# A hybrid encoder on one core: the gates' logarithm moved behind k's convolutions, and an opening with products of ones

## The chip, the cores and the metric

The kernel runs on one core of a Trainium2 chip. The metric is the device time of one execution in microseconds (us), the median of three runs. Five engines work side by side, each through its own queue in order: TensorE (PE; its weight loads are listed apart as PEld), VectorE (DVE), ScalarE (ACT), GpSimd (POOL), and SyncE (SP), which here only issues transfers.

## The reference

A trunk of two layers over 256 tokens of 1024 channels, all in float32. Each layer:

```python
h = rmsnorm(x, norm_w[l]);  proj = h @ w_in[l]
q_a, k_a, v_a, ab_a, z_a, q_b, k_b, v_b, z_b, gate_a, gate_b = split(proj)
# branch a: five-tap convolution and SiLU on q_a, k_a, v_a; q, k of unit length, then
beta = sigmoid(ab[:2])                                  # two directions, eight heads
g = -exp(a_log) * softplus(ab[2:] + dt_bias)            # logarithms of the decays
g = cumsum(g within a chunk)
decay = where(lower, exp(g_i - g_j), 0)
L = where(strict, (kb @ k.T) * decay, 0);  T = inverse(eye + L)   # gated delta rule, both directions
# branch b: differential attention, with rotary positions
lam = exp(sum(lp[0] * lp[1])) - exp(sum(lp[2] * lp[3])) + lambda_init
a = softmax(s0) - lam * softmax(s1)
x = x + (sigmoid(gate_a) * (y_a @ w_pa) + sigmoid(gate_b) * (y_b @ w_pb)) @ w_out
```

A final rmsnorm closes the trunk.

## The kernel before

**Tiling.** Tokens lie in two tiles of 128 rows (`m`, or `c` for chunk; `NM = 2`). A projection takes 512 columns of weights at a time, in four pairs `kp` of row blocks (`kt = 2 kp + k`). Every weight tile `raw` (128 x 1024 float32) is loaded by SP, cast by ScalarE into an upper part `hi` (L308), and VectorE writes the rest, the lower part `lo` (L310). The activations `hT` have an upper and a lower part too, and each product is three: upper x upper, upper x lower, lower x upper. `hi` and `lo` have two buffers, so that a cast waits until TensorE has left the tile before the last.

**The opening (layer 0).** Five products of ones run while the first loads come in; the norm's weights are spread by three products (`norm_row`), then the positions are turned by two 1x1 products into `pos_p` (L435). `opening` norms row tile 0, turns it (`rows`, `split_T`: four transposes each for channels 0 to 511 and 512 to 1023, a ScalarE cast at L234, a VectorE subtraction at L238), and begins the first half of `v_b`'s projection with `products(m, kp, lower)` (L454). An order written by hand ties them together: `mark["proj"]` is the last product, and `behind(x)` queues an instruction behind `x` on the same engine. With `lower` false a pair gives four products, upper and lower activations with upper weights; with `lower` true two, upper activations with lower weights. Between the two pairs of row tile 0 the second row tile is normed and turned.

**A layer's order.** Then come the small parameters, the 32 columns of `ab` (gates), the exponential of their negative size (`ev`, L635), λ (`ls`, L647; `neglam`), k's convolutions in two halves of four heads (`conv`: the copy at L666, four tap steps on VectorE at L670, a Tanh at L676, a product at L681; then transposes and squares), the second half of `v_b`'s projection (`proj_by_tile`, tile `pp_vb`, L369), q's convolution, and q's and k's projections of the attention (`pp_qk`). `v_b`'s second half, row tile by row tile, takes two of four PSUM banks that k's convolutions use as well. One of its weight tiles lies in the place that `B` takes later.

**The gates.** `log_decays()` stands behind `v_b`'s second half. It adds to k's sums of squares (`kss`, which lie beside `ev` in one tile `e_`), takes POOL's power for the lengths (L730), one logarithm over all 40 columns (L732), and makes from them `lnc` (bias of the exponentials) and `glog`; four products with `tri` sum `glog` along the tokens (`grps`, L745); VectorE copies the sums to `grow`, POOL sends them to DRAM (`gdr`), four transposes turn them (`gcps`), and `ngc`, `E_`, `nE` follow. `decays(g, c)` then, for each of four groups of heads and chunk, has POOL fetch `gdr` spread over 128 partitions into `B` (L780), adds `kds`, masks both directions with `affine_select` (L786), and has ScalarE take eight exponentials (L791) with `lnc` as bias; `weigh_k(g, c)` adds the directions and multiplies by k k^T (`kk`, L772, on TensorE). An order `cut` holds the last two fetches behind a mask.

The scheduler takes instructions in the order in which the program names them as their priority, so that a step named earlier goes first where its inputs are there; `behind` and `issue_after` bind it further.

Of the kernel before, what the change touches and what calls it, by code (L numbers as in the profile page):

```python
# [17 lines left out]
P = 128  # L18
# [31 lines left out]
def hybrid_encoder(  # L50
# [219 lines left out]
    def behind(ins):  # L270
        return nullcontext() if ins is None else tc.issue_after(ins)
# [161 lines left out]
    pos_p = ps_p.tile([P, 512], F32, tag="p", name="pos")  # L433
    for m in range(NM):
        mm = T.matmul(pos_p[:, m : m + 1], pos_r[:, m * P : (m + 1) * P], ones[0:1, 0:1], start=True, stop=True)  # L435
        tc.keep_in_program_order(mm)

    def opening(w, evac, places):

        accs = banks2("pp_vb00")
        later, lows = {}, []
        parts = weights(w, C_VB, 512, "vb00", places, ahead=False, later=later, spare=(3,), halved=(0,), late=lows)
        ws = [next(parts), next(parts)]
        tokens(1)

        def products(m, kp, lower):
            terms = [(2 * kp + k, pa, 0) for k in range(2) for pa in range(2)]
            if lower:  # L450
                terms = [(2 * kp + k, 0, 1) for k in range(2)]
            for n_, (kt, pa, pw) in enumerate(terms):
                with behind(mark["proj"]):
                    mark["proj"] = T.matmul(accs[m], hT[kt // 4][:, pa, kt % 4, m * P : (m + 1) * P], ws[kt][1 + pw],  # L454
                                            start=kt == 0 and not n_ and not lower,
                                            stop=kt == KT - 1 and lower).ins

        def rows(m, i, h, **kw):
            split_T(hT[i], heads4(h[:, 512 * i : 512 * i + 512]), m, f"h0{i}", bank_c, **kw)
            mark["turn", m, i], mark["split", m, i] = mark["turn"], mark["split"]  # L460

        h = normed(xt, wb, 0, "n0")
        low = mark["norm", 0][1]
        for high, lo, raw, hi in lows:
            with behind(low):
                low = V.tensor_tensor(lo, raw, hi, ALU.subtract).ins
        rows(0, 0, h, after=(None, low))
        made = norm_tiles("n0", 1)
        norm_factor(xt, 1, *made, range(2), mark["split", 0, 0][0])
        rows(0, 1, h, after=(mark["square", 1, 1], mark["sum"]))  # L470
        mark["proj"] = mark["turn", 0, 1]
        products(0, 0, False)
        products(0, 0, True)
        h = normed(xt, wb, 1, "n0", (None, mark["split", 0, 1][1]), made)
        later[1] = mark["split", 0, 1][0], mark["norm", 1][1]
        ws += [next(parts), next(parts)]
        products(0, 1, False)
        ws += [next(parts), next(parts)]
        at = mark["proj"]
        after = mark["vb00", 2]  # L480
# [12 lines left out]
        mark["later"] = {0: mark["vb00", 3]}  # L493


    for l in range(DEPTH):
# [152 lines left out]
        V.scalar_tensor_tensor(neglam, ls[:, 1:2], -lam0, ls[:, 0:1], ALU.add, ALU.subtract)  # L649


        kq = big.tile([P, NH, NM, 2, P], F32, tag="kq", name=f"kq{l}")
# [67 lines left out]
        gdr = dram.tile([NM, 8, 2, P], F32, tag="gdr", name=f"gdr{l}")  # L720
        lnc = small.tile([P, 2, NM, NH], F32, tag="lnc", name=f"lnc{l}")
        nE = small.tile([P, 4, NH], F32, tag="nE", name=f"nE{l}")
        E_ = small.tile([P, 4, NH], F32, tag="E_", name=f"E_{l}")

        def log_decays():
            kss = e_[:, :, 32:40]
            V.tensor_scalar(kss, ssk, 4.0 * EPS, None, ALU.add)
            kh = small.tile([P, NM, NH], F32, tag="kh", name=f"kh{l}")
            V.tensor_scalar(kh, kss, 1.0 / 16.0, None, ALU.mult)
            G.tensor_tensor(nrm.rearrange("p m h -> p (m h)"), kh.rearrange("p m h -> p (m h)"),  # L730
                            phalf, ALU.pow)
            S.activation(e_, e_, AF.Ln)  # L732
# [22 lines left out]
            ngc = small.tile([P, 4, NH], F32, tag="ngc", name=f"ngc{l}")  # L755
# [3 lines left out]
            V.tensor_tensor(lnc.rearrange("p d c h -> p (d c) h"), lnc.rearrange("p d c h -> p (d c) h"),  # L759
                            ngc, ALU.add)  # L760


        A = big.tile([P, 2, NM, 4, P], F32, tag="A", name=f"A{l}")
# [9 lines left out]
                                              start=True, stop=True).ins  # L773
            return heads4(gp)

        def decays(g, c, after=None):
            hs4 = slice(4 * g, 4 * g + 4)
            dec = B[:, c, hs4].rearrange("p h d i -> p d h i")
            with behind(after):
                G.dma_start(out=B[:, c, hs4].rearrange("p h d i -> p (h d i)"),  # L780
                            in_=gdr[c, hs4].rearrange("h d i -> (h d i)").partition_broadcast(P))
            end = (P - 1) * (1 - c)
            G.tensor_tensor(kds[:, c, hs4], dec[:, c, :, end], lnc[:, c, c, hs4], ALU.add)
            for d in range(2):
                sg = 1 - 2 * d
                mark["cut"] = G.affine_select(  # L786
                    out=dec[:, d], in_=dec[:, d], compare_op=ALU.is_ge, fill=BIG,
                    base=0, pattern=[[0, 4], [sg, P]], channel_multiplier=-sg).ins
                for j4 in range(4):
                    h = 4 * g + j4  # L790
                    S.activation(dec[:, d, j4, :], dec[:, d, j4, :], AF.Exp,  # L791
                                 bias=lnc[:, d, c, h : h + 1])
# [309 lines left out]
        qk_part(0, 0)  # L1102
        decays(0, 0)
        weigh_k(0, 0)
        cut = mark["cut"]
        decays(0, 1)
        weigh_k(0, 1)
        decays(1, 0, cut)
        weigh_k(1, 0)
        decays(1, 1, cut)  # L1110
        weigh_k(1, 1)
        turn_blocks()
        conv("q", C_QA, 1, 1)
# [238 lines left out]
```

## Time and profile before

| | |
|---|---|
| median of 3 runs | 751.38 us (750.87 to 751.71) |
| the profiled execution | 750.2 us |
| its span, first to last instruction | 748.5 us |
| mean granted TensorE clock | 0.997 |
| TensorE busy | 739.9 us (99%) |
| VectorE, ScalarE, POOL busy | 588.6, 475.3, 143.5 us |
| transfers | 135.45 MB, 181 GB/s in the mean |

In the profile a row of a timeline gives start, duration, engine, line, operation, tiles (out<-in), shape, count, and in brackets the idle time of the engine before it and what ended it. A float32 product of 128 x 128 stands in the records as two. Ends of matmuls are modelled, so that durations of neighbours overlap; the distance from start to start is what one costs.

### The profile page before, as it was taken

Reading aid. Unit: us, or ns where it says so; the run is one execution under the profiler, and the core shown is the slowest. Engines: PE = TensorE matmul, PEld = TensorE weight load, DVE = VectorE, ACT = ScalarE, POOL = GpSimd, SP = SyncE. Lnnn points to the kernel's source line nnn. Section 1 sums busy time; section 2 is a strip of 40 time slices with the busy share of each in tenths; the row PEclk is TensorE's granted clock in tenths of the full one; section 3 lists DMA queues with packets and bytes.
Section 4 is the critical chain, followed back from the end, with each engine's and each line's share of the span. In section 5 each row is a group of like instructions: output and inputs, shape, how many; then the busy total and the mean of one; then the engine's idle time right before and its main releaser. Section 6 shows DMA issues by size and latency. Waiting matters only on the chain.

```text
span 748.5 us, 13886 instructions
## 1 busy us (share of the span) xinstructions
PE 739.9 (99%) x5164; PEld 640.8 (86%) x5164; DVE 588.6 (79%) x1109; ACT 475.3 (64%) x1016; POOL 143.5 (19%) x221
## 2 busy tenths in 40 slices
PE   8999999999999999999999999999999999999996
PEld 6999889977888889888889889889778888998885
DVE  8686899999985965578667779999999679537782
ACT  6657675667876576645454677655687758566552
POOL 6000441112022450000000025202110425301000
PEclk9999999999999999999999999999999999999999
DMA  8752767776667462567674358768666747335641
GB/s 261 235 171 80 214 206 214 209 213 194 208 185 178 146 183 83 171 200 248 199 232 141 85 144 257 217 183 228 198 172 195 198 135 231 92 114 202 219 142 56
DMA packets 73733, 135.45 MB, mean 181 GB/s; under 512 B 12944, under 2 KB 13921, under 8 KB 73666
## 3 DMA queue, kind: packets, MB, share of 16 engines
q1 hardware_dynamic: 64750, 113.65, 50.0%
q0 software_dynamic: 7936, 19.35, 9.0%
q10 hardware_dynamic: 980, 1.58, 0.6%
q8 instruction: 40, 0.66, 0.4%
q14 instruction: 27, 0.22, 0.1%
HBM read 125.53 MB, written 9.01 MB: 180 GB/s over the span
## 4 chain that ended last, share of the span: by engine, by line
PE 97%; DMA 1%; issue 1%; DVE 0%; ACT 0%; SPq 0%; POOLq 0%; POOL 0%; DVEq 0%; ACTq 0%
PE pp_vb L369 4%; PE pp_qk L325 4%; PE pp_qk L324 4%; PE pp_qk L326 4%; PE sc L1033 2%; PE pp_o L369 2%; PE pp_za L325 2%; PE pf_v L385 2%; PE pf_k L385 2%; PE pf_v L389 2%; PE pp_gb L324 2%; PE pp_gb L325 2%; PE pp_zb L324 2%; PE pf_k L387 2%; PE pf_k L389 2%; PE pf_q L387 2%
## 5 line engine op out<-in xcount | busy, mean ns | idle before, releaser
L325 PE MATMUL pp_qk<-lo_qk,hT 128*128 128x512 f32 x128 | 50.7, 396 | 0.0
L326 PE MATMUL pp_qk<-hi_qk,hT 128*128 128x512 f32 x128 | 50.0, 390 | 0.0
L310 DVE TENSOR_TENSOR lo_qk<-raw_qk,hi_qk 128x1024 fp32r<-128x1024 f32 x32 | 39.5, 1234 | 9.6 <-ACT hi_qk L308 9.1
L324 PE MATMUL pp_qk<-hi_qk,hT 128*128 128x512 f32 x128 | 45.2, 394 | 0.0
L308 ACT CAST hi_qk<-raw_qk 128x1024 fp32r<-128x1024 f32 x28 | 29.4, 1049 | 23.6 <-PE pp_qk L326 11.8
L1043 ACT ACTIVATE es<-sc,mx 128x256 f32<-128x256 f32 x64 | 29.6, 474 | 19.6 <-DVE mx L1041 19.6
L310 DVE TENSOR_TENSOR lo_pb<-raw_pb,hi_pb 128x1024 fp32r<-128x1024 f32 x16 | 19.6, 1225 | 21.5 <-ACT hi_pb L308 21.2
L387 PE MATMUL pf_q<-hT,hi_q 128*128 128x256 f32 x128 | 36.2, 286 | 0.0
L385 PE MATMUL pf_q<-hT,hi_q 128*128 128x256 f32 x128 | 36.1, 286 | 0.0
L385 PE MATMUL pf_v<-hT,hi_v 128*128 128x256 f32 x128 | 35.8, 285 | 0.0
L385 PE MATMUL pf_k<-hT,hi_k 128*128 128x256 f32 x128 | 35.8, 285 | 0.0
L387 PE MATMUL pf_v<-hT,hi_v 128*128 128x256 f32 x128 | 35.8, 284 | 0.0
L387 PE MATMUL pf_k<-hT,hi_k 128*128 128x256 f32 x128 | 35.6, 283 | 0.0
L389 PE MATMUL pf_q<-hT,lo_q 128*128 128x256 f32 x128 | 34.8, 285 | 0.0
L389 PE MATMUL pf_v<-hT,lo_v 128*128 128x256 f32 x128 | 34.5, 287 | 0.0
L389 PE MATMUL pf_k<-hT,lo_k 128*128 128x256 f32 x128 | 34.3, 283 | 0.0
L670 DVE SCALAR_TENSOR_TENSOR cvq<-pf_q,cw,cvq 128x254 f32<-128x254 f32 (+1 forms) x64 | 29.9, 476 | 1.9 <-ACT cvq L666 1.4
L308 ACT CAST hi_pa<-raw_pa 128x1024 fp32r<-128x1024 f32 x16 | 16.9, 1054 | 22.2 <-PE pp_pa L326 16.0
L670 DVE SCALAR_TENSOR_TENSOR cvk<-pf_k,cw,cvk 128x254 f32<-128x254 f32 (+1 forms) x64 | 28.5, 478 | 2.1 <-ACT cvk L666 1.4
L670 DVE SCALAR_TENSOR_TENSOR cvv<-pf_v,cw,cvv 128x254 f32<-128x254 f32 (+1 forms) x64 | 29.7, 475 | 0.1
L325 PEld LDWEIGHTS pp_qk<-lo_qk,hT 128*128 128x128 f32 x128 | 24.0, 188 | 6.1 <-DVE lo_qk L310 1.3
L310 DVE TENSOR_TENSOR lo_pa<-raw_pa,hi_pa 128x1024 fp32r<-128x1024 f32 x16 | 19.6, 1224 | 11.2 <-ACT hi_pa L308 11.2
(409 smaller groups left out, 2541.2 us busy)
## 6 DMA issues: line engine op xcount, KB each, us to landing
raw_qk<-in_w_in_dram SPq DMA_DIRECT2D x32, 512.0 KB, 4.0
raw_k<-in_w_in_dram SPq DMA_DIRECT2D x16, 512.0 KB, 4.4
raw_q<-in_w_in_dram SPq DMA_DIRECT2D x16, 512.0 KB, 3.8
raw_v<-in_w_in_dram SPq DMA_DIRECT2D x16, 512.0 KB, 3.8
raw_zb<-in_w_in_dram SPq DMA_DIRECT2D x16, 512.0 KB, 3.9
raw_za<-in_w_in_dram SPq DMA_DIRECT2D x16, 512.0 KB, 3.8
raw_ga<-in_w_in_dram SPq DMA_DIRECT2D x16, 512.0 KB, 4.8
raw_pb<-in_w_pb_dram SPq DMA_DIRECT2D x16, 512.0 KB, 3.8
```

The source lines that it names most:

```text
L308: high = (V.tensor_copy if kp in turned else S.copy)(hi[:, :, :n], raw[:, :, :n]).ins
L310: mark[nm, kp] = high, V.tensor_tensor(lo[:, :, :n], raw[:, :, :n], hi[:, :, :n].bitcast(F32), ALU.subtract).ins
L324: T.matmul(o, act[kt // 4][:, 0, kt % 4, ts_], hi, start=kt == 0, stop=False)
L325: T.matmul(o, act[kt // 4][:, 0, kt % 4, ts_], lo, start=False, stop=False)
L326: mark["proj"] = T.matmul(o, act[kt // 4][:, 1, kt % 4, ts_], hi, start=False, stop=kt == KT - 1).ins
L369: mark["proj"] = T.matmul(o, act[kt // 4][:, pa, kt % 4, ts_], ws[kt][1 + pw], start=kt == 0 and n_ == 0, stop=kt == KT - 1 and n_ == 2).ins
L385: T.matmul(o, hi[:, cs], act[kt // 4][:, 0, kt % 4, :], start=first, stop=False, skip_group_check=True)
L387: T.matmul(o, hi[:, cs], act[kt // 4][:, 1, kt % 4, :], start=False, stop=False, skip_group_check=True)
L389: T.matmul(o, lo[:, cs], act[kt // 4][:, 0, kt % 4, :], start=False, stop=done, skip_group_check=True)
L670: V.scalar_tensor_tensor(ca[:, o0:o1], acc[:, b, o0 + sft : o1 + sft], cw[:, j, cb : cb + 1], ca[:, o0:o1], ALU.mult, ALU.add)
L1033: mm = T.matmul(sp[n][:, qt * SEQ : (qt + 1) * SEQ], qkT[h // 4][rows, 0, h % 4, qt * P : (qt + 1) * P], qkT[h // 4][rows, 1, h % 4, :], s ...
L1043: S.activation(es[:, n, qt, :], spv[:, qt, :], AF.Exp, bias=mx[:, n, qt : qt + 1], accum_out=s_all[:, h, n, qt : qt + 1])
```

## The change

*The opening.* Three products of ones with ones, written to unused columns of `pos_p`, stand ahead of the first transposes, and three more behind the first pair's products. The first pair of row tile 0 goes in another order: upper x upper for both row blocks, then upper activations x lower weights, then lower activations x upper weights.

*The gates.* `log_decays` is split. `gates()`, named behind k's convolutions, takes the logarithm of `ev` alone (queued behind the cast of the first weight tile of k's second half), `glog`, the sums, `gdr`, `ngc`, `E_`, `nE`. `lambdas()`, named behind `v_b`'s second half, takes λ's exponential (behind the cast of the second weight tile of k's second half). `spread()` issues the four fetches into `B` and then the eight masks in one go, ahead of `log_decays()`, which keeps k's sums, POOL's power, a logarithm of `kss` alone, and `lnc`. `decays` keeps `kds` and the exponentials, and the order `cut` is gone.

```diff
+        def warm(n):
+            for _ in range(n):
+                with behind(mark["proj"]):
+                    mark["proj"] = T.matmul(pos_p[:, P : 2 * P], ones, ones, start=True, stop=True).ins
+
+        mark["proj"] = mark["pos"]
+
         def products(m, kp, lower):
             terms = [(2 * kp + k, pa, 0) for k in range(2) for pa in range(2)]
-            if lower:
+            if lower is True:
                 terms = [(2 * kp + k, 0, 1) for k in range(2)]
+            elif lower:
+                terms = [(2 * kp + k, pa, pw) for k, pa, pw in lower]
...
+        warm(3)
         rows(0, 0, h, after=(None, low))
         made = norm_tiles("n0", 1)
         norm_factor(xt, 1, *made, range(2), mark["split", 0, 0][0])
         rows(0, 1, h, after=(mark["square", 1, 1], mark["sum"]))
         mark["proj"] = mark["turn", 0, 1]
-        products(0, 0, False)
-        products(0, 0, True)
+        products(0, 0, ((0, 0, 0), (1, 0, 0), (0, 0, 1), (1, 0, 1), (0, 1, 0), (1, 1, 0)))
+        warm(3)
...
-        S.activation(ls, ls, AF.Exp)
...
-            S.activation(e_, e_, AF.Ln)
-            V.scalar_tensor_tensor(ev, a_, 0.0, ev, ALU.max, ALU.add)
+            S.activation(kss, kss, AF.Ln)
             for d in range(2):
                 V.scalar_tensor_tensor(lnc[:, d], ev[:, :, d * 8 : d * 8 + 8], -1.0, kss,
                                        ALU.mult, ALU.subtract)
+            V.tensor_tensor(lnc.rearrange("p d c h -> p (d c) h"), lnc.rearrange("p d c h -> p (d c) h"),
+                            ngc, ALU.add)
+
+        def lambdas():
+            with behind(mark[f"k{l}1", 1][0]):
+                S.activation(ls, ls, AF.Exp)
+            V.scalar_tensor_tensor(neglam, ls[:, 1:2], -lam0, ls[:, 0:1], ALU.add, ALU.subtract)
+
+        def gates():
+            with behind(mark[f"k{l}1", 0][0]):
+                S.activation(ev, ev, AF.Ln)
+            V.scalar_tensor_tensor(ev, a_, 0.0, ev, ALU.max, ALU.add)
             glog = small.tile([P, NM, 16], F32, tag="glog", name=f"glog{l}")
...
+        def spread():
+            for g in range(2):
+                for c in range(NM):
+                    hs4 = slice(4 * g, 4 * g + 4)
+                    G.dma_start(out=B[:, c, hs4].rearrange("p h d i -> p (h d i)"),
+                                in_=gdr[c, hs4].rearrange("h d i -> (h d i)").partition_broadcast(P))
+            for g in range(2):
+                for c in range(NM):
+                    dec = B[:, c, 4 * g : 4 * g + 4].rearrange("p h d i -> p d h i")
+                    for d in range(2):
+                        sg = 1 - 2 * d
+                        G.affine_select(
+                            out=dec[:, d], in_=dec[:, d], compare_op=ALU.is_ge, fill=BIG,
+                            base=0, pattern=[[0, 4], [sg, P]], channel_multiplier=-sg)
...
         conv("k", C_KA, 0, 1)
+        gates()
         for _ in proj_by_tile(hT, wl, C_VB + 512, evac_v(1), f"vb{l}1", places2, spare=range(4),
...
             pass
+        lambdas()
+        spread()
         log_decays()
```

More of the change, by code (lines that the diff above doesn't have):

```diff
@@ L435, in hybrid_encoder @@
         mm = T.matmul(pos_p[:, m : m + 1], pos_r[:, m * P : (m + 1) * P], ones[0:1, 0:1], start=True, stop=True)
+        mark["pos"] = mm.ins
         tc.keep_in_program_order(mm)
@@ L454, in products @@
                     mark["proj"] = T.matmul(accs[m], hT[kt // 4][:, pa, kt % 4, m * P : (m + 1) * P], ws[kt][1 + pw],
-                                            start=kt == 0 and not n_ and not lower,
-                                            stop=kt == KT - 1 and lower).ins
+                                            start=kt == 0 and not n_ and lower is not True,
+                                            stop=kt == KT - 1 and lower is True).ins
         def rows(m, i, h, **kw):
@@ L722, in hybrid_encoder @@
         nE = small.tile([P, 4, NH], F32, tag="nE", name=f"nE{l}")
+        ngc = small.tile([P, 4, NH], F32, tag="ngc", name=f"ngc{l}")
         E_ = small.tile([P, 4, NH], F32, tag="E_", name=f"E_{l}")
@@ L754, in log_decays @@
                 T.transpose(gc_ps[:, dc * 8 : dc * 8 + 8], grow[:, dc, :], ident[:8, :8])
-            ngc = small.tile([P, 4, NH], F32, tag="ngc", name=f"ngc{l}")
             V.tensor_scalar(ngc, gc_ps[:, :32].rearrange("p (c h) -> p c h", c=4), -1.0, None, ALU.mult)
@@ L758, in log_decays @@
             V.tensor_scalar(nE, E_, -1.0, None, ALU.mult)
-            V.tensor_tensor(lnc.rearrange("p d c h -> p (d c) h"), lnc.rearrange("p d c h -> p (d c) h"),
-                            ngc, ALU.add)
         A = big.tile([P, 2, NM, 4, P], F32, tag="A", name=f"A{l}")
@@ L774, in gram, with decays @@
             return heads4(gp)
-        def decays(g, c, after=None):
+        def spread():
[12 more added lines that the diff above has]
+                            base=0, pattern=[[0, 4], [sg, P]], channel_multiplier=-sg)
+        def decays(g, c):
             hs4 = slice(4 * g, 4 * g + 4)
             dec = B[:, c, hs4].rearrange("p h d i -> p d h i")
-            with behind(after):
-                G.dma_start(out=B[:, c, hs4].rearrange("p h d i -> p (h d i)"),
-                            in_=gdr[c, hs4].rearrange("h d i -> (h d i)").partition_broadcast(P))
             end = (P - 1) * (1 - c)
@@ L784, in decays @@
             for d in range(2):
[L785 to L788, printed above, removed]
                 for j4 in range(4):
@@ L1104, in hybrid_encoder @@
         weigh_k(0, 0)
-        cut = mark["cut"]
         decays(0, 1)
         weigh_k(0, 1)
-        decays(1, 0, cut)
+        decays(1, 0)
         weigh_k(1, 0)
-        decays(1, 1, cut)
+        decays(1, 1)
         weigh_k(1, 1)
```

1 line of the change is left out of this document (removed).

## The prediction

> **What bounds the kernel now.** I read the page's busy line and chain, then who TensorE waited for, then the clock by stretches, then the opening engine by engine, then the stretch of k's and q's convolutions.
>
> ```profile
> PE 739.9 (99%) x5164; PEld 640.8 (86%) x5164; DVE 588.6 (79%) x1109; ACT 475.3 (64%) x1016; POOL 143.5 (19%) x221
> ...
> PE 97%; DMA 1%; issue 1%; DVE 0%; ACT 0%; SPq 0%; POOLq 0%; POOL 0%; DVEq 0%; ACTq 0%
> ```
>
> TensorE is 97% of the chain that ended last. Its waits for others, all of them in the list:
>
> ```profile
> PE idle L410 <- DVE ones L407: 1.1, 1, 1.1
> PE pp_vb L454 <- ACT hT L234: 0.4, 1, 0.4
> PE pp_vb L454 <- DVE hT L238: 0.3, 1, 0.3
> ```
>
> They sum to 1.8 us of a 748.5 us span, and all lie in the opening. So the gates, which the change moves, end no wait of TensorE: whatever leaves ScalarE or VectorE there comes off work that is hidden already. What the wait list can't show is a slow matmul. The stretches (columns: five engines' busy time, then granted clock, DMA share, GB/s) show one such place:
>
> ```profile
> 9.00:10.00 1.00, 0.65 (x3) 0.45 (x3) 0.57 (x2) 1.00 (x5) 0.00 (x0) 0.79 1.07 412
> 10.00:11.00 1.00, 1.00 (x4) 0.81 (x3) 0.74 (x3) 1.00 (x2) 0.87 (x2) 0.50 1.03 398
> ...
> 12.00:13.00 1.00, 1.00 (x4) 0.72 (x4) 1.00 (x2) 0.55 (x1) 1.00 (x1) 0.50 1.18 324
> 13.00:14.00 1.00, 1.00 (x10) 0.91 (x9) 1.00 (x2) 0.15 (x1) 1.00 (x1) 1.00 0.67 248
> ```
>
> The clock falls to half at 10.0 − 0.42 = 9.58 us (0.79 is 0.42 us at one half) and is back at 13.0: 3.4 us at half rate, which is 1.7 us of lost matmul time if nothing else had been late. The matmuls around it:
>
> ```profile
> 6.29 0.60 PE L435 MATMUL pos<-ones,pos_r 1*128 1x1 f32 x4
> 6.89 1.31 PE L227 MATMUL pt_h<-ident,h_n 128*128 128x128 f32 x8
> 8.62 0.49 PE L454 MATMUL pp_vb<-wA_vb,hT 128*128 128x512 f32 x1 [0.42 <-ACT hT L234]
> 9.46 2.42 PE L454 MATMUL pp_vb<-wA_vb,hT 128*128 128x512 f32 x5 [0.35 <-DVE hT L238]
> ...
> 13.21 1.04 PE L227 MATMUL pt_h<-ident,h_n 128*128 128x128 f32 x8
> 14.00 0.70 PE L454 MATMUL pp_vb<-wktm_vb,hT 128*128 128x512 f32 x2
> 14.54 1.55 PE L454 MATMUL pp_vb<-wvtm_vb,hT 128*128 128x512 f32 x6
> 15.93 0.39 PE L454 MATMUL pp_vb<-wA_vb,hT 128*128 128x512 f32 x1
> ```
>
> Between 6.3 and 9.4 us TensorE did the position's 1x1 products, eight transposes and one 128x512 product. In the slow stretch five 128x512 take 2.42 us with the last one's end, about 0.43 us from start to start; after it six take 15.93 − 14.54 = 1.39 us, 0.23 us each. From 14.54 on there is no gap.
>
> **The change, part by part. The opening, order of products.** Before, the second product needs the lower part of hT, so 8.62 to 9.46 holds one product. After, the upper parts of both rows and the lower parts of the weights go first: four products need only what is there at 8.62 and end near 9.5, when the lower part (8.73 + 0.68 = 9.41 below) is there. At full clock six products end at 8.62 + 6 × 0.23 = 10.0, against 9.46 + 5 × 0.43 = 11.6 before.
>
> ```profile
> 7.99 0.58 ACT L234 CAST hT<-pt_h 128x512 fp32r<-128x512 f32 x1
> 10.17 1.05 ACT L308 CAST wktm_vb<-raw_vb 128x1024 fp32r<-128x1024 f32 x1
> 8.73 0.68 DVE L238 TENSOR_TENSOR hT<-pt_h,hT 128x512 fp32r<-128x512 f32 x1
> 12.23 1.22 DVE L310 TENSOR_TENSOR wktm_vb<-raw_vb,wktm_vb 128x1024 fp32r<-128x1024 f32 x1
> 86.38 0.89 PE kk L772 x8
> ```
>
> The 1.7 us aren't all won. The next weights' upper part lands at 10.17 + 1.05 = 11.22, so the next four products run 11.27 to 12.2, the transposes (1.04 for eight, 13.21 to 14.25 by ends, 0.8 by starts) to about 13.1, and the next two wait for the lower part of that weight, 12.23 + 1.22 = 13.45. They then start at 13.48 where they started at 14.00: the gain is 0.5 us, and 0.6 us by the next group (13.95 for 14.54). VectorE is late next; it has work back to back there.
>
> **The opening, products of ones.** Two sets of three. Four fp32 128x128 products (two records each) took 0.89 us, so three cost 0.67 us at full clock. The first set starts when the position products are issued (6.29 + four steps of about 0.12 = 6.8) and ends at 7.45, so the transposes move from 6.89 to 7.45. ScalarE takes their result at 7.99, having been busy to then; the first four transposes would be readable near 8.2 (four starts of 0.11 us and some 0.3 us behind the last). That is 0.2 us later for everything in the opening, and the gain falls from 0.6 to 0.4 us. The second set fits between 10.2 and 11.4, where TensorE would wait for ScalarE: nothing, if the clock is up. Whether the filling holds the clock no row of before shows; bounds: yes, −0.6 (no delay of the transposes), and no, below. I take **−0.4 us**.
>
> The Trainium skill, "TensorE: Matmul & The Clock Gate", Part 1, says that a free-running window of 3413 ns decides between half and full rate, and that its phase varies from run to run; the 3.4 us above agree. Its Part 4 says transposes don't count as busy; if so, the filling is what decides.
>
> **The gates: ScalarE.** Before, one logarithm per layer takes 40 columns; after, one takes 32 (behind the first cast of the second half of k) and one 8 (in the old place). That puts a second pair of table loads into each layer, one before the new logarithm and one before the next Tanh. λ's Exp moves behind the logarithm; if it needs a load of its own, that is a third, which the Tanh load shares.
>
> ```profile
> 73.84 1.28 ACT L732 ACT_TABLE_LOAD   x1
> 75.13 0.27 ACT L732 ACTIVATE ge<-ge 128x80 f32<-128x80 f32 x1
> 76.68 1.28 ACT L676 ACT_TABLE_LOAD   x1
> ```
>
> So 2 × 1.28 + 0.2 = 2.8 us of ScalarE per layer, at this place:
>
> ```profile
> 36.50 0.48 ACT L666 ACTIVATE cvk<-pf_k,cw 128x256 f32<-128x256 f32 x1 [1.25 <-PE pf_k L389]
> 37.04 1.05 ACT L308 CAST hi_k<-raw_k 128x1024 fp32r<-128x1024 f32 x1
> 39.92 1.05 ACT L308 CAST hi_k<-raw_k 128x1024 fp32r<-128x1024 f32 x1 [0.88 <-PE pf_k L387]
> 41.37 0.42 ACT L676 ACTIVATE thk<-cvk 128x256 f32<-128x256 f32 x1 [0.40 <-DVE cvk L670]
> ...
> 38.13 1.23 DVE L310 TENSOR_TENSOR lo_k<-raw_k,hi_k 128x1024 fp32r<-128x1024 f32 x1
> ...
> 43.92 1.23 DVE L310 TENSOR_TENSOR lo_k<-raw_k,hi_k 128x1024 fp32r<-128x1024 f32 x1 [0.27 <-ACT hi_k L308]
> ...
> 49.89 1.22 DVE L310 TENSOR_TENSOR lo_q<-raw_q,hi_q 128x1024 fp32r<-128x1024 f32 x1 [0.78 <-ACT hi_q L308]
> ```
>
> The first load and the logarithm (1.5 us) fall into the 1.25 us idle before 36.50: 0.3 us late. The tile cast at 37.04 has its lower part at 38.13 + 1.23 = 39.36, and TensorE turns to it when it frees the buffer before (the cast at 39.92 waits for that): 0.6 us of slack, so no stall. The Tanh load falls before 41.37, into 0.4 us of idle: 0.9 us late. Here the queue behind counts: VectorE's next product for that head waits for the Tanh, and convolution steps of later heads stand behind it.
>
> The Trainium skill, "ScalarE: Activation LUTs", What ACT_TABLE_LOAD costs, puts a switch at 1283 ns and a drain of 1380 ns. By it the two loads would be an estimated 2.8 us longer per layer, and the sum, less the idle time and slack named here, about +2.5 us instead of −0.4. The trace differs: the load ends at 75.12, the logarithm starts at 75.13, with no drain, so that rule gets no chance of its own.
>
> **The gates: VectorE and TensorE.** Moved into k's stretch: five small operations of some 0.2 us, the copy of the sums' bank at 0.7 us, in all 1.6 us; the same leaves q's. TensorE's eight small fp32 records and eight transposes cost the same in either place. The tight spot is the second half of v's last product: its bank is k's second one, freed by the convolution of k's fourth head.
>
> ```profile
> 51.37 3.47 DVE L670 SCALAR_TENSOR_TENSOR cvk<-pf_k,cw,cvk 128x254 f32<-128x254 f32 x8
> 54.52 0.70 PE L369 MATMUL pp_vb<-wvb,hT 128*128 128x512 f32 x2
> ```
>
> Eight steps, alternating between the fourth head and the next half's first; the fourth head's last is the sixth, done two steps of some 0.45 us before 54.84, near 53.9: slack 0.6 us. VectorE's shift there is at most 0.9 + 1.6 = 2.5 us, less the 0.78 us of idle before 49.89 and 0.27 us before 43.92 = 1.45; less the slack, 0.85 us per layer (the second layer's work is the same), 1.7 in all. At the other end the moved operations wait behind k's steps and the price is zero. I take **+0.3 us** for both layers, nearer the low end, because no moved result is wanted before 60 us.
>
> **The gates: POOL, the transfers and what follows.**
>
> ```profile
> L791 ACT ACTIVATE B<-B,lnc 128x128 f32<-128x128 f32 x32 | 9.9, 391 | 1.3 <-POOL B L786 1.3
> L786 POOL TENSOR_SCALAR_AFFINE_SELECT B<-B 128x512 f32<-128x512 f32 x8 | 7.2, 916 | 0.0
> L325 PEld LDWEIGHTS pp_qk<-lo_qk,hT 128*128 128x128 f32 x32 | 6.0, 188 | 1.5 <-DVE lo_qk L310 0.4
> ...
> POOL nrm L730 <- DVE kh L729: 112.9, 2, 58.8
> ...
> 45.00:65.00 20.00, 20.00 (x127) 17.91 (x126) 15.74 (x35) 11.87 (x37) 0.00 (x0) 1.00 0.30 87
> 85.00:105.00 20.00, 20.00 (x152) 19.08 (x151) 18.11 (x32) 16.15 (x44) 9.91 (x14) 1.00 0.79 243
> ```
>
> Four broadcasts and eight masks (7.2 us) go ahead of the norm's power on POOL. POOL had idled 58.8 us before that power, whose result v's placing takes far later: nothing. On the transfer engines they leave a stretch at 0.79 for one at 0.30: nothing on SP's loads. The 32 exponentials (9.9 us) need not wait for them any more and can start near 77 instead of 91, spreading ScalarE's and VectorE's work out of the fullest 20 us (18.1 of VectorE). Weight loads of TensorE there waited 0.4 us for lower parts; at most that, 0.35 us per layer with the slowed matmuls, comes back. I take **−0.3 us** of 0 to −0.7.
>
> **Sum.** −0.4 + 0.3 − 0.3 = −0.4 us. On the profiled execution (750.2 us, a span of 748.5 and 1.7 around it): 749.8. The shown runs' median is 1.2 above it, so 751.0 there. A measurement of this kernel tells a change from none at about 0.2%, 1.5 us: 749.9 to 752.9 counts as the same.
>
> **The rivals.** *Slower, by VectorE's queue in k's stretch:* the Tanh load holds VectorE, the moved operations come before k's steps instead of behind, and v's second half starts late in both layers. 1.7 us as worked out; with a third load (1.28 us) or the sums' copy ahead of a weight's lower part (0.7 against 0.6 us of slack), another 0.3 to 0.5 per layer: +2.5 − 0.4 = 753.5. It decides once the shift reaches some 1.6 us per layer over what idle time takes up. For it: 18 of 20 us of VectorE's time are taken nearby. Against: 15.7 of 20 in this very stretch. Chance 0.18.
>
> *The clock falls all the same:* three products are too few. Then two of the six and the second set of ones run at half rate: 9.6 + 2.6 × 0.43 + 1.3 = 12.0, the four products end near 13.4, transposes 14.3, and the next group starts 0.2 us later than the old 14.54. +0.2 with the middle at nothing: 751.6. For it: 0.67 us of 3.4 is little. Against: the reordered products fill another 0.9 us of the same window. Chance 0.12.
>
> *Faster, by a half-rate stretch elsewhere:* a clock window that starts later would lay its 3.4 us over matmuls that nothing else holds up, and its removal is then worth the full 1.7 us, −1.9 in all with a little of the middle: 749.5. For it: the shown runs, 750.87 to 751.71, all lie above the profiled 750.2, by 0.7 to 1.5. Against: a window beginning after 9.5 holds back-to-back products and shouldn't be throttled. The free-running window of the Trainium skill (page and part named above) is this rule. Chance 0.18.
>
> **How the numbers follow.** Forecast as summed 0.52, own range 750.1 to 752.2. The point is its 751.0. The range reaches from the faster rival's 749.4 to 753.0, leaving out most of the slower one and a little below. Faster by over 0.2%: the faster rival and the rim of the forecast, 0.20; slower: the second, 0.18; the same: the rest, 0.62.
>
> **What would show it.** Right: a granted clock of 1.00 from 9 to 14 us, the wvtm group starting near 14.1, four table loads in each layer's k and q stretches, exponentials before 85 us, and TensorE's wait list no longer than before. Wrong: a TensorE wait at v's second half (near 54 and 420), weight loads waiting for lo_k or lo_q, or half rate in the opening.

## The result, and the profile after

The changed kernel takes 759.6 us (median of 4 runs, 758.0 to 761.9), the kernel before 751.1 beside it: a ratio of 1.0114, interval 1.0086 to 1.0142. It is 8.5 us slower; 751.0 was forecast, within 749.4 to 753.0.

The page of the changed kernel, busy line and chain:

```profile
PE 743.7 (98%) x5176; PEld 642.8 (85%) x5176; DVE 587.6 (78%) x1109; ACT 481.7 (64%) x1022; POOL 142.8 (19%) x221
...
PE 89%; DVE 4%; ACT 3%; DMA 2%; issue 2%; POOLq 0%; POOL 0%; DVEq 0%; ACTq 0%
```

ScalarE has 6.4 us more work, 5.1 of it four more table loads of 1.28 us, but it is busy for 64% of the span. What is not TensorE now holds 11% of the chain where it was 3%. What TensorE waited for (total, times, longest):

```profile
PE pf_q L385 <- ACT stg L597: 2.5, 2, 1.4
...
PE pp_qk L325 <- DVE lo_qk L310: 0.9, 3, 0.3
PE pf_q L389 <- DVE lo_q L310: 0.8, 1, 0.8
...
PE pf_q L385 <- ACT hi_q L308: 0.3, 1, 0.3
```

These new rows all lie in one place, the attention's q and k products (`pp_qk`) and q's second convolution half (`pf_q`). Comparing the starts of the same matmul in both traces: TensorE is 0.1 us early when q's convolution begins (60.2 us before), 3.9 late when v's begins (112.6), 4.7 at the end of the layer; in layer 1 it goes to 7.5 at v's convolution (478.5) and 8.6 at the end. Most of it, 6.8 us by these starts, is lost between q's first half and v's convolution (the list above counts idle time alone, 4.5 us there); 0.8 per layer is lost at the attention's score products, and is gone in every run below whose exponentials stand later.

ScalarE in that stretch of the changed kernel:

```profile
81.75 1.05 ACT L308 CAST hi_qk<-raw_qk 128x1024 fp32r<-128x1024 f32 x1 [0.66 <-PE pp_qk L326]
82.74 0.40 ACT L816 ACTIVATE B<-B,lnc 128x128 f32<-128x128 f32 x1
...
83.80 2.14 ACT L816 ACTIVATE B<-B,lnc 128x128 f32<-128x128 f32 x7
87.26 1.05 ACT L308 CAST hi_q<-raw_q 128x1024 fp32r<-128x1024 f32 x1 [1.32 <-DMA raw_q<-in_w_in_dram]
88.21 0.98 ACT L816 ACTIVATE B<-B,lnc 128x128 f32<-128x128 f32 x3
...
89.41 1.56 ACT L816 ACTIVATE B<-B,lnc 128x128 f32<-128x128 f32 x5
...
91.23 0.68 ACT L816 ACTIVATE B<-B,lnc 128x128 f32<-128x128 f32 x2
91.81 0.56 ACT L597 COPY stg<-pp_qk 128x512 f32<-128x512 f32 x1
```

and in the kernel before:

```profile
85.74 0.59 ACT L586 COPY stg<-pp_qk 128x512 f32<-128x512 f32 x1 [2.02 <-PE pp_qk L326]
...
91.51 1.27 ACT L791 ACTIVATE B<-B,lnc 128x128 f32<-128x128 f32 x4
```

Before, the copy `stg`, which frees a bank of `pp_qk`, ran the moment the products were done, and no exponential of `B` stood ahead of it. After, 18 of 32 stand ahead of it in ScalarE's program. TensorE's side in the changed kernel:

```profile
87.68 0.39 PE L326 MATMUL pp_qk<-hi_qk,hT 128*128 128x512 f32 x1
...
90.79 0.28 PE L389 MATMUL pf_q<-hT,lo_q 128*128 128x256 f32 x1
92.43 0.39 PE L385 MATMUL pf_q<-hT,hi_q 128*128 128x256 f32 x1 [1.36 <-ACT stg L597]
```

The products were done at 88.1; the copy started at 91.81, and the convolution wanted the bank near 91.1. The Trainium skill, "PSUM — Partial Sum Buffer", Engine vs sequencer instructions, says that ScalarE's queue is strictly first in, first out; these rows agree.

GpSimd's queue after:

```profile
69.89 1.16 POOL L771 DMA_DIRECT2D gdr<-grow  x2 [49.77 <-DVE grow L768]
75.24 2.21 POOL L797 DMA_DIRECT2D B<-gdr  x4 [4.19 <-DMA gdr<-grow]
...
86.69 0.49 POOL L812 TENSOR_TENSOR kds<-B,lnc 128x4 f32<-128x4 f32 x3
```

The sums reached DRAM only at 75 us, and the four fetches went out in a row. The stretches after (last columns: clock, DMA share, GB/s):

```profile
9.00:10.00 1.00, 1.00 (x4) 0.86 (x5) 0.67 (x1) 1.00 (x4) 0.00 (x0) 1.00 1.03 397
...
45.00:65.00 20.00, 20.00 (x127) 17.90 (x126) 15.66 (x35) 11.93 (x37) 0.00 (x0) 1.00 0.31 95
```

The clock's dip is gone. The stretch of few transfers is as it was (0.31): no fetch moved there. From 78 to 86 the transfer engines were full:

```profile
78.00:82.00 4.00, 4.00 (x23) 3.26 (x21) 2.52 (x4) 3.33 (x6) 3.92 (x3) 1.00 0.98 250
82.00:86.00 4.00, 3.67 (x15) 2.62 (x15) 3.96 (x9) 3.60 (x10) 2.90 (x5) 1.00 0.99 393
```

and in the kernel before:

```profile
78.00:82.00 4.00, 4.00 (x22) 3.00 (x21) 3.54 (x7) 2.06 (x4) 1.21 (x2) 1.00 0.56 174
82.00:86.00 4.00, 4.00 (x25) 3.21 (x25) 3.67 (x10) 1.74 (x4) 1.15 (x2) 1.00 0.64 164
```

The load of q's weights that SP issued at 76.69 us took 10.5 us to land; the same load took 4.4 before (issued at 75.33).

### The profile page after: what moved, and what is told of

The parts are those of the page before. It is cut to its first block, busy times and chain, and to the rows that moved or that the text cites. A ratio compares the mean times of both kernels' runs of the same rounds, so it can differ in the third digit from the quotient of the medians.

```text
span 757.1 us, 13925 instructions
## 1 busy us (share of the span) xinstructions
PE 743.7 (98%) x5176; PEld 642.8 (85%) x5176; DVE 587.6 (78%) x1109; ACT 481.7 (64%) x1022; POOL 142.8 (19%) x221
## 4 chain that ended last, share of the span: by engine, by line
PE 89%; DVE 4%; ACT 3%; DMA 2%; issue 2%; POOLq 0%; POOL 0%; DVEq 0%; ACTq 0%
PE pp_vb L369 4%; PE sc L1058 2%; PE pp_qk L324 2%; PE pp_qk L326 2%; PE pp_qk L325 2%; PE pp_o L369 2%; PE pp_zb L324 2%; PE pf_k L385 2%; PE pp_gb L325 2%; PE pp_za L325 2%; PE pp_gb L324 2%; PE pp_za L324 2%; PE pf_k L387 2%; PE pf_k L389 2%; PE pp_ga L324 2%; PE pp_ga L325 2%
## 5 line engine op out<-in xcount | busy, mean ns | idle before, releaser
L310 DVE TENSOR_TENSOR lo_qk<-raw_qk,hi_qk 128x1024 fp32r<-128x1024 f32 x32 | 39.6, 1237 | 10.7 <-ACT hi_qk L308 10.3
```

The lines of the kernel that those rows point to most:

```text
L310: mark[nm, kp] = high, V.tensor_tensor(lo[:, :, :n], raw[:, :, :n], hi[:, :, :n].bitcast(F32), ALU.subtract).ins
```

## The experiments

Each kernel is told from the kernel before ("before") or from the changed kernel ("after"); times are medians, ratios are to the kernel before on the same chip, with 95% intervals in brackets.

### Which half of the change

*The opening alone* (before, with the new opening):

```diff
+        warm(3)
         rows(0, 0, h, after=(None, low))
...
+        products(0, 0, ((0, 0, 0), (1, 0, 0), (0, 0, 1), (1, 0, 1), (0, 1, 0), (1, 1, 0)))
+        warm(3)
```

> The opening's part alone; the rest as before. The changed kernel's trace has the clock at full rate from 6.4 us on, yet TensorE stands only 0.1 us earlier at 18.8 us than before. Theory one (the rest alone makes the loss): 0 to -0.4 us, 750.7 to 751.1. Rival (the ones delay the first transposes, and that costs more in other phases of the clock's window): +0.5 us or more. Either way no wait at 80 to 100 us.

750.9 us, 1.0004 (0.9994 to 1.0014): nothing that shows.

*The gates alone* (after, with the old opening):

> The gates' part alone; the opening as before. If the loss lies wholly there: 759 to 761 us, with TensorE 4.7 us late at z's projections and 8.7 us late at the end, and the same waits near 82 to 92 us. If opening and gates only lose together (the earlier TensorE meets a late cast), it would come to 752 to 755.

759.7 us, 1.0118 (1.0103 to 1.0134): all of it.

### Which step of the gates, one taken back at a time

*Fetches two by two, masks between:*

```diff
         for g in range(2):
             for c in range(NM): G.dma_start(...)
-        for g in range(2):
             for c in range(NM): ... G.affine_select(...)
```

> The changed kernel, but the fetches of B go two by two, the masks of the first pair ahead of the second pair's fetches. Theory A (four fetches of 512 KB in a row starve the weight loads: the queue of the weights moved no byte from 78 to 80 us): q's load lands in time, the stalls at 87.7 and 88.6 us go, and the ones that follow from ScalarE's wait for that load: -2 to -4 us in layer 0, 755 to 757. Theory B (ScalarE's queue: the second pair of table loads and the exponentials that now stand ahead of casts and of the copies that free banks): 758 to 760, the stalls stay.

758.4 us, 1.0102 (1.0087 to 1.0117). *Fetches and masks back in `decays`, with the order `cut`:*

```diff
-        spread()
+        decays(1, 0, cut)    # fetch, kds, masks, exponentials, as before the change
```

> The changed kernel, but fetches and masks stand in decays again with the old hold, so gates, lambdas and the split logarithm are the change that is left. Theory A and any theory that blames the early fetch and the early exponentials: 751 to 752. Theory of the table loads (two more in each layer, at 1.28 us each, with the second pair between casts of q's and qk's weights): 753 to 756, with lo_qk late for the third and fourth weight tile near 82 and 85 us.

758.4 us, 1.0107 (1.0086 to 1.0127). *Without the logarithm of k's sums, and so without the second pair of table loads (the sums are scaled instead, so that this kernel computes something else from k's lengths):*

```diff
-            S.activation(kss, kss, AF.Ln)
+            V.tensor_scalar(kss, kss, 0.1, None, ALU.mult)
```

> The changed kernel without the logarithm of k's sums (a product with 0.1 on VectorE in its place, so lnc lacks that term): the second pair of table loads, at 75.4 and 77.7 us, is gone, 2.6 us of ScalarE per layer. Theory B2: the stalls of lo_qk near 82 and 85 us go and what follows from them, 752 to 754. Theory B1: the exponentials still stand ahead of the copies, so the wait for stg near 90 us stays, 756 to 759.

760.7 us, 1.0135 (1.0111 to 1.0159). Each of these three looks worth 1.2 us at most. That reading was too quick: the last runs show that the fetches and the loads were hidden under what follows. *Exponentials of `B` late:*

```diff
+                    mark["qkT", s_, i, m] = S.mul(qkT[i]...).ins
...
+                    with behind(mark["qkT", 0, 0, 0]):
                         S.activation(dec[:, d, j4, :], ..., AF.Exp, bias=lnc[...])
```

> The changed kernel, with the 32 exponentials of each layer queued behind the first copy of turned q (the place that they have before the change) and nothing else held. Theory B1 (the exponentials, ready 10 us earlier, stand in ScalarE's queue ahead of the copies that free TensorE's banks and of casts): the waits of q's products for stg and of lo_q go, about -3 us per layer, 752 to 754. Theory B2 (the second pair of table loads): 757 to 759, the stalls of lo_qk at 82 and 85 us and 452 and 456 us stay, and later ones too.

756.2 us, 1.0064 (1.0041 to 1.0087), the wait for `stg` gone. *The two last edits together:*

> Both: the exponentials held as in the run before last and no logarithm of k's sums (lnc lacks that term). If loads and exponentials are the whole loss: 750 to 752, and no wait of TensorE in 80 to 100 us. If something else of the gates costs (the small products moved into q's convolution, the transfers), a rest of 2 us or more stays: 753 or above.

754.0 us, 1.0049 (1.0033 to 1.0065).

### The split of the logarithm alone

*Before, with `ev`'s logarithm split off and queued behind the cast in k's second half, sums and fetches named where they were:*

```diff
+        def early_log():
+            with behind(mark[f"k{l}1", 0][0]):
+                S.activation(ev, ev, AF.Ln)
...
-            S.activation(e_, e_, AF.Ln)
+            S.activation(kss, kss, AF.Ln)
```

> The kernel before, with the logarithm split alone: that of the gates behind the first cast of k's second half, that of k's sums where it was; sums, fetches, masks and opening as before. It has all the extra table loads, and its fetches wait for the sums as before. Theory B2: 755 to 758. Theory B1 in its strict form (only an early fetch makes early exponentials): 751 to 752. But here too ScalarE's program has 24 of the exponentials ahead of the first copy of q's bank, where before it has none; if that order is what costs, 754 to 758 with waits for stg, however late the fetch.

759.7 us, 1.0120 (1.0102 to 1.0138). Without a burst of fetches (they go out in pairs, at 73.8 and 79.9 us), the whole loss is there. The sums are early here too, at 67.3 us as in the changed kernel (78.2 before): they are named where they were, but their input is ready earlier. 24 of 32 exponentials stand ahead of the first copy `stg` in ScalarE's program, and q's casts between them. Here TensorE's largest wait is for the lower parts made from those casts, and none for the copy is listed:

```profile
PE pf_q L389 <- DVE lo_q L310: 3.4, 3, 1.5
```

*The same with the exponentials of `B` late:*

> The kernel before with the logarithm split and nothing else of the change (as in the run of that edit alone, 759.7 us), and the 32 exponentials of a layer held behind the first copy of q's and k's products. Both logarithms with their table loads stay. Theory 'exponentials' (the split costs time only because the exponentials get an earlier place in ScalarE's program, ahead of the copies that free TensorE's banks and of q's casts): 751 to 753 us, no wait of TensorE over 0.6 us in q's and k's products. Theory 'table loads' (two more loads and the logarithms' own time press on ScalarE): 757 to 760 us, the exponentials' place being no matter.

753.5 us, 1.0044 (1.0028 to 1.0061): by the ratios the place makes 5.7 us of it, with both pairs of table loads kept.

### The fetches, and an artefact

*After, exponentials late, fetches as before the change:*

> The changed kernel with both of its suspects taken back: the 32 exponentials of a layer stand behind the first copy of q's and k's products (as in the run with the late exponentials, 756.2 us), and the four fetches into B go as before the change, each ahead of its own masks and the last two behind a mask. Both logarithms, the early sums and the new opening stay. Theory 'transfers' (what the late exponentials leave, some 3 to 5 us, is q's weights arriving late because four 512 KB fetches in a row keep SP's queue from moving): q's loads land as before, 751 to 752.5 us, and no cast of q's upper parts waits over 1 us for its load. Theory 'order' (what is left is the sums', k k^T's and the copies' new places ahead of q's and k's products): those stay, so 754 to 756 us.

752.9 us, 1.0026 (1.0016 to 1.0036). *The same without the second logarithm:*

> The kernel of 752.9 us (the change with late exponentials and the fetches of before), without the logarithm of k's sums: the sums are scaled instead, so that the second pair of table loads of a layer is gone and what is computed from k's lengths in the weights differs. It tells what makes up the last 1 to 2 us above the kernel before. Theory 'table loads': 2.8 us of ScalarE per layer leave the fullest stretch, 750.5 to 751.5 us. Theory 'order' (the sums', the k k^T's and the second half of q's new places): 752 to 753.5 us.

751.7 us, but from 750.5 to 758.4, 1.0027 (1.0011 to 1.0044): inconclusive. Its profiled execution, one of the long ones, shows why, in ScalarE's rows:

```profile
89.68 0.22 ACT L834 ACTIVATE kds<-kds 128x16 f32<-128x16 f32 x1 [3.45 <-POOL kds L800]
89.80 0.57 ACT L597 COPY stg<-pp_qk 128x512 f32<-128x512 f32 x1
```

The order that held `B`'s exponentials had let the one of `kds` slip ahead of the copy, where it waited for GpSimd and, behind it, for the fetch. ScalarE idled there 2.3 us in the run of 756.2 and 3.8 in that of 752.9, both layers together. So these runs may carry a cost of their own; the section after this one takes it away. *Sums early in fact (after, exponentials late, the sums' tiles in the other set of banks):*

```diff
-            gr_ps = bank_c(f"grps{l}")
+            gr_ps = bank(f"grps{l}")      # gc_ps likewise
```

> The changed kernel with the late exponentials, and with the two tiles of the sums (grps, gcps) in the other set of PSUM banks, so that the sums need not wait for a bank of k's transposes: they stand inside k's second half in TensorE's program, some 15 us earlier, and the four fetches can follow near 55 us, where the transfer engines were 30% busy. Theory 'transfers': the burst meets a half-empty stretch, q's loads land in time, 750.5 to 752 us. If moving the burst only moves the harm (to the loads of q's first half, 60 to 70 us), 753 to 756, with casts of q's first half waiting for loads. Theory 'order': TensorE's sums and transposes are still ahead of q's products, 753 to 756, but without a cast of q waiting for a load.

752.3 us, 1.0025 (1.0016 to 1.0034). The sums moved from 67 to 39.5 us. TensorE paid 1.4 us inside k's convolutions, 2.3 in all by v's second half, and got about 1 back later. The fetches gained less than the sums: `B` lies where a weight tile of `v_b`'s second half lies, and GpSimd waited for the products with it:

```profile
61.28 2.20 POOL L797 DMA_DIRECT2D B<-gdr  x4 [16.88 <-PE pp_vb L369]
```

*The burst alone (before, with the fetches in a row, then the masks):*

```diff
+        spread()
-            with behind(after):
-                G.dma_start(out=B[:, c, hs4]..., in_=gdr[c, hs4]...)
```

> The kernel before with one edit: the four fetches into B in a row, then the eight masks, as the change does it; logarithm, sums and opening as before. In the engines' programs little else moves (the 32 exponentials stay behind the copies of q's and k's products). Theory 'transfers': q's loads come late as in the changed kernel, 752.5 to 755 us, with casts of q's upper parts waiting 1 to 4 us for a load. Theory 'order': 750.5 to 751.5, no change.

751.3 us, 1.0008 (1.0000 to 1.0017): on the kernel before, a burst costs 0.6 us, 0 to 1.3 by the interval.

### Both exponentials held

Here the exponential of `kds` stands behind the last one of `B`:

```diff
+                        mark["exp"] = S.activation(dec[:, d, j4, :], ...).ins
...
+            with behind(mark["exp"]):
                 S.activation(kds, kds, AF.Exp)
```

*After, whole:*

> The changed kernel whole (its opening, both logarithms, early sums, four fetches in a row), with two orders in ScalarE's program: the 32 exponentials of B of a layer behind the first copy out of q's and k's turned products, and the exponential of kds behind the last of them. In the earlier run that held B's exponentials alone (756.2 us) that of kds had moved ahead of the copy that frees TensorE's bank, and ScalarE waited 2.3 us there for POOL's kds. Theory 'place' (the loss is what stands ahead of the copies and casts in ScalarE's program, and nothing else): 750.5 to 752 us, no wait of TensorE for stg. Theory 'place and burst': the wait for kds is gone, and q's weights still come late, 752.5 to 754.5 us.

755.6 us, 1.0068 (1.0049 to 1.0087). TensorE's waits in that run:

```profile
PE pf_q L389 <- DVE lo_q L310: 1.7, 2, 0.9
PE pf_q L385 <- ACT hi_q L308: 1.5, 2, 0.8
```

and ScalarE's row behind them:

```profile
87.53 1.04 ACT L308 CAST hi_q<-raw_q 128x1024 fp32r<-128x1024 f32 x1 [4.10 <-DMA raw_q<-in_w_in_dram]
```

The copy is no longer late; q's weights are. *With the fetches as before the change:*

> The changed kernel with the fetches as before the change, and the same two orders. Theory 'place': 750.5 to 751.5 us, as with the burst. Theory 'place and burst': 750.5 to 751.5 us, 2 us less than with the burst.

752.8 us, 1.0030 (1.0019 to 1.0042): by the ratios the burst is worth 2.9 us here. *The split alone:*

> The kernel before with the logarithm split alone, and the same two orders. Theory 'place': 750.5 to 751.5 us, the table loads costing nothing. Theory 'table loads': some of the 753.5 us of the run with B's exponentials alone held stays, 752 to 753.5 us.

752.5 us, 1.0019 (1.0010 to 1.0029): 7.6 us of the split's 9.0 were the place of the exponentials. *Sums early in fact:*

> The changed kernel with the sums' tiles in the other set of banks (sums and fetches some 15 us earlier) and the same two orders. The run with B's exponentials alone held had 752.3 us and no wait for kds, since the fetches had landed by then. Theory 'place': nothing was held there, so 752 to 752.6 as before; what it pays is TensorE's sums inside k's convolutions (1.4 us there). If kds's place mattered there too: 751.

752.5 us, 1.0024 (1.0015 to 1.0034), as without the order on `kds`. That order changed nothing in the whole change either (1.0064 without, 1.0068 with it) or with the old fetches (1.0026, 1.0030); it took 1.9 us off the split alone (1.0044, 1.0019). *The run of 752.8 without the second logarithm:*

> The kernel of e16_old_late_all (752.8 us) without the logarithm of k's sums, which are scaled instead: the second pair of table loads of a layer (1.28 us each, near 75 and 77 us) is gone, TensorE's, POOL's and SP's programs are the same instruction for instruction, and what is computed from k's lengths differs. Theory 'table loads': the last 2 us are ScalarE's and so VectorE's lateness behind the loads, TensorE's waits for lo_qk (0.6 us) shrink, 750.5 to 751.5 us. Theory 'order': TensorE's sums and products of k with k ahead of q's products make them, 752 to 753 us.

750.1 us, 0.9993 (0.9984 to 1.0002): level with the kernel before. All waits of TensorE but the first of `ones`:

```profile
PE pp_vb L464 <- DVE wktm_vb L310: 0.2, 1, 0.2
```

So the loads, with the logarithm that needs them, are worth 2.8 us by the ratios. One of the waits that went with them:

```profile
PE pp_qk L325 <- DVE lo_qk L310: 0.6, 2, 0.4
```

The casts of `hi_qk` suggest how two loads, for which TensorE waited nowhere before, come to cost. In the run of 752.8:

```profile
74.16 1.05 ACT L308 CAST hi_qk<-raw_qk 128x1024 fp32r<-128x1024 f32 x1
75.23 1.28 ACT L742 ACT_TABLE_LOAD   x1
76.52 0.21 ACT L742 ACTIVATE ge<-ge 128x16 f32<-128x16 f32 x1
77.50 1.28 ACT L685 ACT_TABLE_LOAD   x1 [0.76 <-DVE cvq L679]
...
79.47 1.04 ACT L308 CAST hi_qk<-raw_qk 128x1024 fp32r<-128x1024 f32 x1
```

and in the kernel before:

```profile
72.76 1.06 ACT L308 CAST hi_qk<-raw_qk 128x1024 fp32r<-128x1024 f32 x1
73.84 1.28 ACT L732 ACT_TABLE_LOAD   x1
...
75.61 1.06 ACT L308 CAST hi_qk<-raw_qk 128x1024 fp32r<-128x1024 f32 x1 [0.20 <-PE pp_qk L326]
76.68 1.28 ACT L676 ACT_TABLE_LOAD   x1
```

Before, a cast stood between the loads; 2.85 us lay from cast to cast. After the split none does, and 5.31 us lie between: the next `lo_qk` is late. That the place of this cast is the cause is argued from these rows; no run put the cast back with the loads kept.

### The account

| taken back, in this order | ratio | worth |
|---|---|---|
| nothing (after) | 1.0114 | |
| the burst of fetches | 1.0107 | 0.5 us |
| the exponentials' place (`B` and `kds`) | 1.0030 | 5.8 us |
| the second pair of loads | 0.9993 | 2.8 us |

The first step can't be told from nothing (the two intervals overlap almost wholly); the other two can. In another order the shares differ: the place first gives 3.5 us (1.0068), the burst then 2.9; the loads first give nothing (1.0135, intervals overlapping). I read this so: they delay the same copies and casts, and the longest hides the others. What is left of the change at the end, the new opening, the early logarithm with its loads, λ's exponential, the early sums, moves the time by nothing that shows. No run beats the kernel before.

## Why the prediction was wrong

**The failed step is "The gates: POOL, the transfers and what follows"**, taken as −0.3 us, 0 to −0.7. The gates as a whole, summed there at nothing (+0.3 − 0.3), cost 8.9 us alone (1.0118). Three of the step's claims fell.

*The exponentials "can start near 77 instead of 91, spreading ScalarE's and VectorE's work out of the fullest 20 us".* They started at 82.7, and that is what cost most: 5.8 us by the table. The step counted ScalarE's 9.9 us as work that may lie anywhere, and asked only what the moved step waits for. It did not name what stands behind it on its own engine: the copies of TensorE's banks and q's casts. I had asked that of the loads and of GpSimd's power, not of the largest block that the change sets free.

*The fetches "leave a stretch at 0.79 for one at 0.30: nothing on SP's loads".* The share of 45 to 65 us was the wrong row. The sums use banks that k's transposes hold, ran at 67 us, and the fetches went out at 75.24, into 0.98 and 0.99. The price was 0.5 to 2.9 us. Even where the sums did run at 39.5 us, the fetches went out only at 61.28, when `v_b`'s products had left the place of `B`, so most of 45 to 65 us was never open to them; nothing was won (752.5).

*Its bounds held gains only.* The prediction had read that TensorE waited for nothing in that stretch, so there was little to win and much to lose; no row of the moved work's neighbours was asked for a loss. (The range's lower end, 749.4, is 0.1 below the faster rival's own 749.5, which changes nothing.)

**"The gates: ScalarE"** held at the place that it looked at. The pair of loads in k's stretch cost nothing: the last run keeps it and is level. λ's Exp took a load of its own, which the Tanh behind it shared, as the step allowed, and that cost nothing either:

```profile
35.19 1.28 ACT L756 ACT_TABLE_LOAD   x1
36.48 0.26 ACT L756 ACTIVATE ge<-ge 128x64 f32<-128x64 f32 x1
...
39.00 1.28 ACT L751 ACT_TABLE_LOAD   x1
40.30 0.20 ACT L751 ACTIVATE ls<-ls 128x2 f32<-128x2 f32 x1
```

What it missed is the pair left behind at 75 us. It counted as paid for, since it had stood there before; its neighbours had not stayed, and taking it away gave 2.8 us.

**"The gates: VectorE and TensorE"** (+0.3) and the slower rival, at v's second half: neither happened. TensorE has no wait at 54 or 420 us. The rival's sign was right, its mechanism and its size were not.

**The opening** (−0.4): the clock, once up, stayed up through the opening, here and in all 14 profiles with it (of six with the old one, it fell to half again in three), and the groups moved, as the rows of the changed kernel show.

```profile
6.42 0.60 PE L435 MATMUL pos<-ones,pos_r 1*128 1x1 f32 x4
6.95 0.94 PE L452 MATMUL pos<-ones 128*128 128x128 f32 x6
7.72 1.04 PE L227 MATMUL pt_h<-ident,h_n 128*128 128x128 f32 x8
9.00 1.66 PE L464 MATMUL pp_vb<-wA_vb,hT 128*128 128x512 f32 x6 [0.24 <-ACT hT L234]
...
14.45 1.55 PE L464 MATMUL pp_vb<-wvtm_vb,hT 128*128 128x512 f32 x6
```

The transposes start 0.83 us later, not 0.56 (0.13 of it from the position's products), and the group forecast near 14.1 starts at 14.45 (14.54 before). Two things take the rest. In the run of the opening alone TensorE was 0.5 us early up to 100 us and had lost it at 110, waiting for `lo_qk`. And the first step to full clock comes at another time in each execution: in the 14 profiles with this opening between 4.2 and 10.9 us. Where it comes late, the ones run at half rate ahead of the transposes. The profile of the run of 752.9 us:

```profile
6.34 1.01 PE L435 MATMUL pos<-ones,pos_r 1*128 1x1 f32 x4
7.28 1.65 PE L452 MATMUL pos<-ones 128*128 128x128 f32 x6
8.72 1.92 PE L227 MATMUL pt_h<-ident,h_n 128*128 128x128 f32 x8
```

Against the kernel before, TensorE is then 1.4 us late at 18.9 us (three profiles), and else between 0.6 early and 0.15 late (eleven). The mean over the 14 is 0.1 us late. With the old opening five more profiles lie between 0.4 early and 0.1 late, and the two of them with full clock at 10.7 and 10.8 us are only 0.1 late, so what makes the late step costly here is the new opening. The term should have been zero, between −0.6 and +1.4; the forecast weighed one phase of the clock as if it were all.

**What the forecast's own test said.** The clock at 1.00, four table loads and the first exponentials before 85 us came as "right" while the time was wrong; only "TensorE's wait list no longer than before" caught it. The first three tell whether the steps happen, and the list alone whether they cost.

## What to carry to other kernels

When a change makes a large block ready earlier, ask what stands behind it on its engine: in an in-order queue work that could run early also takes the place of work that must run on time, and an engine that is 64% busy can still hold the bound one. If the order comes from a scheduler's priorities, look at the new order of each engine's program and not only at what was edited, and fix the place of such blocks. Taking suspects back one at a time shows only the longest of several delays that overlap; take back two and three together before calling one harmless.

## What the runs showed of the hardware that was not expected

- Full clock began anywhere from 4.2 to 10.9 us, and stretches at half rate last 3.41 us. The Trainium skill, "TensorE: Matmul & The Clock Gate", Part 1, calls the window free-running; the spread agrees. An opening is worth its mean over this phase.
- A stall can be followed by half rate. Behind the late weights of the 755.6 us run, in its profiled execution of 757.3, the clock fell to half from 91.0 to 94.4 us (columns as above). Stalls of the same size in the changed kernel were followed by none, so what decides it is not shown:

```profile
86.00:90.00 4.00, 2.46 (x12) 1.58 (x10) 1.78 (x4) 2.46 (x5) 3.81 (x8) 1.00 0.50 161
...
92.00:94.00 2.00, 2.00 (x11) 2.00 (x11) 2.00 (x6) 0.08 (x1) 0.00 (x0) 0.50 0.59 188
```

- An exponential behind a logarithm loaded a table again (39.00 us above). The Trainium skill, "ScalarE: Activation LUTs", Table sets: the hidden batching unit, has both in one set, with a single load; the trace differs.
